# Channel shuffle on one core: five SBUF buffers of 40 KB a partition in place of 38 KB

## The chip, the core and the metric

The kernel runs on one core of one Trainium2 chip. The metric is the device time of one execution in microseconds (us); less is better. Three timed runs of the kernel before gave 316.11, 316.14 and 316.18 us, a median of 316.14 us.

## What is computed

The input `x` is an fp32 tensor of 16 x 64 x 64 pixels with 256 channels each, 67.11 MB. The 256 channels are 8 groups of 32. The reference swaps the two channel axes of every pixel:

```python
x = x.reshape(batch, h, w, groups, channels_per_group)
x = x.transpose(0, 1, 2, 4, 3)
x = x.reshape(batch, h, w, c)
```

There is no arithmetic. Each pixel is 1 KB in and 1 KB out, and 65,536 pixels make 512 pixels for each of the 128 partitions of SBUF. So "q KB a partition" and "q pixels a partition" are the same number here, and the whole job is 512 KB a partition in and 512 KB a partition out.

## The kernel before

The tensor is flattened and cut into pieces. A piece of q KB takes 128 x q pixels that lie together in HBM; partition p gets q of them, so each partition's part is one run of q KB in HBM, and the runs of neighbouring partitions follow one another.

The list `_SLOTS` (line 12) names the pieces. Each inner list is one slot, that is, one pair of buffers: an `in_tile` and an `out_tile`, both as large as the biggest slot. Slot 1 holds two pieces, 4 and 8 KB; slot 2 holds one of 28 KB; then twelve slots hold one piece of 38 KB each; the last holds 16 KB. That makes 16 pieces. `_IN_BUFS` is 2 and `_OUT_BUFS` is 3, so five buffers of 38 KB a partition are in SBUF.

For every piece there are three steps:

- a load (line 55), a DMA from HBM to `in_tile`, issued by SyncE's queue (SP);
- a copy (line 57) on VectorE (DVE), from `in_tile` to `out_tile`, which reads the channels as (group, channel in the group) and writes them as (channel in the group, group);
- a store (line 61), a DMA from `out_tile` to HBM, issued by ScalarE's queue (ACT).

The order on each engine is the order of the program (`manual_schedule`). Nothing else runs but four small memsets at the start. Three waits tie the steps together. A copy waits for its load and, from the fourth slot on, for the store that last used its `out_tile`, three slots back. A load waits from the third slot on for the copies that last read its `in_tile`, two slots back. A store waits for its copy. Loads and stores lie in two hardware queues, q1 and q10, that are served by the same 16 DMA engines; each DMA of 128 partitions gives every engine 8 rows, one descriptor a row, and one small write that raises the semaphore.

Of the kernel before, what the change touches and what calls it, by code (L numbers as in the profile page):

```python
# [1 line left out]

# [4 lines left out]


F32 = mybir.dt.float32
P = 128  # L10

_SLOTS = [[4, 8], [28]] + [[38]] * 12 + [[16]]
_IN_BUFS = 2
_OUT_BUFS = 3


@with_exitstack
def kernel(
    ctx: ExitStack,
    tc: tile.TileContext,  # L20
    x: bass.AP,
    groups: bass.AP,
    out: bass.AP,
):
    nc = tc.nc
    b, h, w, c = x.shape
    G = int(groups)
    CPG = c // G
    assert G * CPG == c
    assert sum(map(sum, _SLOTS)) * P == b * h * w  # L30
    biggest = max(map(sum, _SLOTS))

    x_flat = x.rearrange("b h w c -> (b h w c)")
    out_flat = out.rearrange("b h w c -> (b h w c)")

    in_pool = ctx.enter_context(tc.tile_pool(name="in_pool", bufs=_IN_BUFS))
    out_pool = ctx.enter_context(tc.tile_pool(name="out_pool", bufs=_OUT_BUFS))

    def rows(flat, first, q):

        return flat[first * c : (first + P * q) * c].rearrange("(p f) -> p f", p=P)

    ctx.enter_context(tc.manual_schedule(engines=None))
    first = 0
    for parts in _SLOTS:
        in_tile = in_pool.tile([P, biggest * c], F32, name="in_tile")
        out_tile = out_pool.tile([P, biggest * c], F32, name="out_tile")
        at = 0
        pieces = []
        for q in parts:  # L50
            pieces.append((q, first, slice(at * c, (at + q) * c)))
            first += P * q
            at += q
        for q, start, cols in pieces:
            nc.sync.dma_start(out=in_tile[:, cols], in_=rows(x_flat, start, q))  # L55
        for q, start, cols in pieces:
            nc.vector.tensor_copy(  # L57
                out=out_tile[:, cols].rearrange("p (i j g) -> p i j g", j=CPG, g=G),
                in_=in_tile[:, cols].rearrange("p (i g j) -> p i j g", g=G, j=CPG),
            )  # L60
            nc.scalar.dma_start(
                out=rows(out_flat, start, q), in_=out_tile[:, cols]
            )


# [1 line left out]
_INS = ['x', 'groups']  # L67
_OUTS = [((16, 64, 64, 256), 'float32')]

_NUMBERS = {'groups': 8}  # L70


# [26 lines left out]
```

## Time and profile before

| | |
|---|---|
| timed runs, median | 316.14 us (316.11 to 316.18) |
| profiled execution, first to last instruction (span) | 314.4 us |
| lying around the span, median less span | 1.7 us |
| VectorE busy | 119.0 us, 16 copies |
| one 38 KB copy | 8791 ns |
| bytes moved | 134.22 MB, 427 GB/s over the span |
| DMA queues' share of the 16 engines | q1 49.8%, q10 49.4% |
| 38 KB load, issue to landing | 37.0 us |
| 38 KB store, issue to landing | 42.6 us |

The profile is of one execution of its own, and its page gives the span but no device time beside it; the median of the timed runs is what a new time is held against. A busy share of VectorE is time in which a copy ran. The DMA's busy share is the mean over the core's 16 DMA engines. The trace also holds one record for each DMA packet (here one row of one partition, or one semaphore write) with its start, size and duration; 4608 of them belong to the two queues.

### The profile page before, as it was taken

The page shows a single profiled execution, that of the slowest core. Times are in us where ns is not written, and L with a number is a line of the kernel's source. Part 1 is how long each engine was busy: PE and PEld are TensorE (multiplying, and loading weights), DVE is VectorE, ACT ScalarE, POOL GpSimd, SP SyncE. Part 2 cuts the span into 40 slices and gives each one's busy share as a digit, 9 for nine tenths or more (in the row PEclk, how much of TensorE's full clock was granted, in tenths as well). Part 3 has the DMA queues.
Part 4 walks back from the last instruction along what each step waited for, and adds up shares of the span by engine and source line. Part 5 has one row for each costly group of instructions (what it writes and reads, how often), then busy time and mean ns, then how long its engine had stood idle before and what let it go on. Part 6 is the DMA issues. An engine that isn't in the chain of part 4 may idle for free.

```text
span 314.4 us, 132 instructions
## 1 busy us (share of the span) xinstructions
DVE 119.0 (38%) x16; POOL 0.2 (0%) x4
## 2 busy tenths in 40 slices
DVE  2081907309109109019028028037046055065400
POOL 0000000000000000000000000000000000000000
DMA  7999999999999999999999999999999999999997
GB/s 317 405 441 416 435 416 483 401 465 406 450 421 446 426 436 436 401 470 396 475 396 475 396 470 401 470 401 470 401 450 421 446 426 436 436 417 450 429 421 321
DMA packets 4608, 134.22 MB, mean 427 GB/s; under 512 B 512, under 2 KB 512, under 8 KB 768
## 3 DMA queue, kind: packets, MB, share of 16 engines
q1 hardware_dynamic: 2304, 67.11, 49.8%
q10 hardware_dynamic: 2304, 67.11, 49.4%
HBM read 67.11 MB, written 67.11 MB: 427 GB/s over the span
## 4 chain that ended last, share of the span: by engine, by line
DMA 76%; DVE 19%; issue 0%; SPq 0%; DVEq 0%
DMA in_tile<-in_x_dram 76%; DVE out_tile L57 19%; SPq L55 0%; DVEq L57 0%
## 5 line engine op out<-in xcount | busy, mean ns | idle before, releaser
L57 DVE COPY out_tile<-in_tile 128x9728 f32<-128x9728 f32 (+4 forms) x16 | 119.0, 7440 | 179.4 <-DMA in_tile<-in_x_dram 179.4
L80 POOL MEMSET const-uint8-127<- 128x1 uint8 x1 | 0.1, 103 | 0.0
L80 POOL MEMSET const-bfloat16-1.0<- 128x1 bf16 x1 | 0.1, 102 | 0.0
L80 POOL MEMSET const-float32-1.0<- 128x1 f32 x1 | 0.1, 100 | 0.0
L80 POOL MEMSET const-float32-0.0<- 128x1 f32 x1 | 0.1, 99 | 0.2 <-issue 0.2
## 6 DMA issues: line engine op xcount, KB each, us to landing
in_tile<-in_x_dram SPq DMA_DIRECT2D x12, 4864.0 KB, 37.0
out_dram<-out_tile ACTq DMA_DIRECT2D x12, 4864.0 KB, 42.6
in_tile<-in_x_dram SPq DMA_DIRECT2D x1, 3584.0 KB, 14.7
out_dram<-out_tile ACTq DMA_DIRECT2D x1, 3584.0 KB, 30.9
in_tile<-in_x_dram SPq DMA_DIRECT2D x1, 2048.0 KB, 30.4
out_dram<-out_tile ACTq DMA_DIRECT2D x1, 2048.0 KB, 15.2
in_tile<-in_x_dram SPq DMA_DIRECT2D x1, 1024.0 KB, 5.4
out_dram<-out_tile ACTq DMA_DIRECT2D x1, 1024.0 KB, 25.0
```

Of the source, the lines that this page charges most:

```text
L57: nc.vector.tensor_copy(out=out_tile[:, cols].rearrange("p (i j g) -> p i j g", j=CPG, g=G), in_=in_tile[:, cols].rearrange("p (i g j) -> ...
L80: nc = _bacc.Bacc("TRN2", target_bir_lowering=False, num_devices=1)
```

## The change

One line differs: the twelve slots of 38 KB and the last of 16 KB become eleven slots of 40 KB and a last one of 32 KB. The first three pieces stay.

```diff
-_SLOTS = [[4, 8], [28]] + [[38]] * 12 + [[16]]
+_SLOTS = [[4, 8], [28]] + [[40]] * 11 + [[32]]
 _IN_BUFS = 2
 _OUT_BUFS = 3
```

The five buffers grow from 38 to 40 KB a partition, 200 KB in all. The 16 pieces become 15. The order of the steps, the queues and the waits are the same.

## The prediction

> **What bounds the kernel now.** I read the page's first three parts first. The line of the DMA's busy share is the main one: nine tenths or more (9) in every slice but the first and the last.
>
> ```profile
> span 314.4 us, 132 instructions
> DVE 119.0 (38%) x16; POOL 0.2 (0%) x4
> DMA  7999999999999999999999999999999999999997
> q1 hardware_dynamic: 2304, 67.11, 49.8%
> q10 hardware_dynamic: 2304, 67.11, 49.4%
> ```
>
> The queues' shares add to 99.2% of 314.4 us, or 311.9 us. Only 2.5 us of an engine's span are not transfer. VectorE has 38%. The view of windows (length, VectorE busy, POOL, clock, DMA share, GB/s) shows where the rest lies.
>
> ```profile
> 0.00:1.00 1.00, 0.00 (x0) 0.20 (x4) 1.00 0.00 0
> 1.00:2.00 1.00, 0.00 (x0) 0.00 (x0) 1.00 0.37 45
> 2.00:49.10 47.10, 18.50 (x4) 0.00 (x0) 1.00 1.00 423
> 71.30:278.20 206.90, 79.14 (x10) 0.00 (x0) 1.00 1.00 433
> 278.20:294.50 16.30, 8.72 (x1) 0.00 (x0) 1.00 1.01 434
> 294.50:312.00 17.50, 3.87 (x1) 0.00 (x0) 1.00 0.98 424
> 313.00:314.40 1.40, 0.00 (x0) 0.00 (x0) 1.00 0.00 0
> ```
>
> The DMA stands idle for 1.7 us at the start (first packet at 1.75 us) and 1.2 us at the end (last packet ends at 313.28 us). In between it is full, also in the writes-only stretch after the last load has landed (294.5 on). The timeline says the same from VectorE's side: each 38 KB copy starts 22.99 us after the one before ((278.19 - 71.31) / 9), and VectorE idles about 14.2 us before each, for its load.
>
> ```profile
> 71.31 8.75 DVE L57 COPY out_tile<-in_tile 128x9728 f32<-128x9728 f32 x1 [13.40 <-DMA in_tile<-in_x_dram]
> 278.19 8.73 DVE L57 COPY out_tile<-in_tile 128x9728 f32<-128x9728 f32 x1 [14.21 <-DMA in_tile<-in_x_dram]
> 294.54 3.87 DVE L57 COPY out_tile<-in_tile 128x4096 f32<-128x4096 f32 x1 [7.62 <-DMA in_tile<-in_x_dram]
> ```
>
> The chain that ended last gives VectorE 19%. That is no cost that a faster copy would return: while those copies run, the engines move other rows at full rate. Three things set the time: bytes over the engines' rate, overhead per packet, and idle DMA at the ends.
>
> **The change, term by term.** Bytes: unchanged, 512 KB a partition each way. Head: the pieces of 4, 8 and 28 KB, their addresses, copies and issues are the same, so the 1.7 us before the first packet stay.
>
> Packets: the packet records give 611 ns for a 16 KB row and 1439 ns for a 38 KB row (medians). Neighbouring packets of one engine overlap by some 4 ns in these records: in the steady part a 38 KB row follows the last after 1435 ns and a 16 KB row after 607 ns. The difference, 828 ns for 22,528 bytes, is 0.03675 ns a byte; 16,384 bytes are then 602.2 ns, which leaves 4.8 ns a row that do not grow with its size. A semaphore write takes 6 ns of the engine. One DMA pair less (16 pieces to 15) takes from each engine 8 read rows, 8 write rows and two semaphore writes: 16 x 4.8 + 2 x 6 = 89 ns. By these numbers a steady 38 KB tile is 16 x 1435 + 12 = 22.97 us, against 22.99 measured, and a 40 KB tile will be 16 x 1510 + 12 = 24.18 us. Gain: 0.09 us. A 40 KB row is 5% beyond the largest one in the trace; I take the straight line, since it holds from 4 KB (159 ns) to 38 KB.
>
> Read stalls: write rows show none (38 KB: 1439 median, 1460 longest). Read rows do, early only. The 38 KB reads lose 0.54 us per engine over their median, nearly all of it before 36 us; 0.36 us of that is one event at 33 us, when all 16 engines' reads took 1.7 to 1.85 us. From 36 to 313 us there is next to nothing. These are reads that the change resizes, so this term can go to zero (-0.54) or grow. I take it as unchanged, because the order of rows there (short writes of 4, 8 and 28 KB between long reads) stays, and keep -0.54 and +0.54 as ends.
>
> Row pitch: 40 KB and 32 KB are rounder distances between the rows that the engines read side by side. The nearest row is the last load of before, whose rows are 16 KB apart, a power of two: all its 128 reads took 611 ns, none more. I take 0.
>
> The Trainium skill, "DMA: Bandwidth & Descriptors", section "Latency and other measured facts", speaks against round pitches: it reports 207 GB/s at 512 KiB between rows, 164 at 2 MiB, and 214 with padding. If its mildest loss, 3%, held for the eight 32 KB read rows of 1.21 us, an estimate from that page is +0.3 us and a total of 316.4 us; the 16 KB reads above speak for 0.
>
> Copies, on VectorE: (8791 - 3873) / (9728 - 4096) = 0.873 ns an element, so a 40 KB copy takes 8791 + 512 x 0.873 = 9.24 us and the 32 KB one 3873 + 4096 x 0.873 = 7.45 us. Counted as nothing: 24.18 - 9.24 leaves 14.9 us idle for each tile, and the loads and stores in flight keep the DMA engines full beside it.
>
> Tail: this cover must be checked, since the last copy grows from 3.87 to 7.45 us and nothing loads beside it. A steady tile moves 76 KB a partition in 22.99 us, 0.3025 us a KB. When the last load landed (294.5), writing went on until 313.28: 18.8 us, or 62 KB, of which 16 were the last piece's own and 46 were older stores. These last 13.9 us; the copy and about 1 us from issue to first byte take 4.9; so 9 us of cover were left over (in the packet records the last store's first row starts at 307.99, 8.6 us after it could). Loads and stores alternate row by row, as the packet records show, so the last load's stretch of before loaded 16 and stored 38, and the lead of loads over stores fell from 84 to 62 KB. After, it loads 32 and stores 40: a lead of at least 84 falls to 76, and without the last piece's own 32 leaves 44 KB of older stores, 13.3 us. Less 7.45 + 1, that is a margin of 4.8 us. No gap opens, and the end of the last store with its 1.2 us behind it is as before. If the cover were gone entirely, the cost would be up to 8.5 us.
>
> Waits: an `out_tile` is asked for again three tiles later, 3 x 24.18 = 72.5 us after the copy into it began; its store is issued 9.2 us into that time and lands about 42.6 x 40/38 = 45 us after issue, so some 18 us are left over. A load is issued when the copy two slots back ends; its predecessor then still has some 14 us to go, so SP's queue of loads never runs dry.
>
> Sum: 314.4 - 0.09 = 314.3 us of span; with the same 1.7 us around it, 316.14 - 0.09 = 316.05 us.
>
> **Rivals.** A measurement of this kernel can tell about 0.2%, 0.63 us, from no change.
>
> *Slower: the long reads stay slow.* The first two 38 KB tiles' 256 reads lost 8.6 us together, 33.5 ns each. If 40 KB and 32 KB rows kept meeting this through the run, 96 reads per engine would lose 3.2 us in place of 0.54: +2.7 - 0.09, or 318.7 us. It is visible beyond a mean of 13 ns a read (96 x 13 = 1.26 = 0.63 + 0.54 + 0.09). For it: the stalls of the start are not explained by the trace, and the pitch is rounder. Against it: 38 KB reads lose nothing from 36 us on, 16 KB reads nothing at all. Chance 0.18, nearer to the threshold as likely as at the full price.
>
> *Slower: the tail opens.* The margin goes from about 9 to 4.8 us. If the last load lands over 4.8 us later against the stores than reckoned, every further microsecond is idle DMA: at 6 us, 1.2 us, or 317.3 us. Against it: the same reckoning gives the last stretch of before as 22.97 x 54/76 = 16.3 us, as measured. Chance 0.07.
>
> *Faster: the read stalls go.* Without them, -0.54 - 0.09 gives 315.5 us, just at the threshold; to pass it, the stalls of the first 28 KB reads (0.26 us per engine) would have to shrink too. Chance 0.10.
>
> That the change doesn't do what it says can be left aside: the order of instructions per engine shows eleven copies, loads and stores of 10240 elements and one of 8192, with the rest the same.
>
> **How the numbers follow.** No visible change, 0.65, at 316.05 us; faster 0.10; slower 0.18 + 0.07 = 0.25. The range for 8 in 10: down to 315.4 (stalls gone, and a little more), up to 317.4 (half of the slow reads' price, or the tail open by 1.2 us). Outside lie about 0.05 below and 0.12 above.
>
> **What would show it.** Right: copies of 40 KB that start 24.18 us apart, VectorE idle 14.9 us before each; 433 GB/s in the middle; the last load lands near 290 us (76 KB at 0.3025, 23.0 us, before the last packet's end at 313.2), the last copy takes 7.45 us and the DMA share stays at 1.00 behind it; queue packets 2160 in place of 2304. Wrong: steady tiles over 24.3 us apart (slow reads), a hole in the DMA share between the last copy's start and the last store (tail), or 40 KB rows that take more than 1514 ns each.

## The result and the profile after

The changed kernel's median is 317.85 us (nine runs, 316.32 to 319.23), against 316.17 us for the kernel before (nine runs, 316.02 to 317.47). The ratio is 1.0046, 95% interval 1.0024 to 1.0068. Slower by about half a percent, and with a spread of 2.9 us: the shortest run of the change is near the kernel before, the others trail upward.

The page of the profiled execution after (its device time was 317.25 us), parts 1 to 3:

```profile
span 315.5 us, 126 instructions
DVE 118.9 (38%) x15; POOL 0.2 (0%) x4
DMA  8999999999999999999999999999999999999996
q1 hardware_dynamic: 2160, 67.11, 49.7%
q10 hardware_dynamic: 2160, 67.11, 49.2%
```

The shares of the two queues add to 98.9% of 315.5 us, 312.0 us. It was 311.9 before: the engines have no more to do, on average. The view of windows (columns as before) shows the place:

```profile
73.00:267.00 194.00, 74.04 (x8) 0.00 (x0) 1.00 1.00 433
290.00:312.00 22.00, 7.32 (x1) 0.00 (x0) 1.00 0.99 429
312.00:313.00 1.00, 0.00 (x0) 0.00 (x0) 1.00 0.08 33
313.00:314.00 1.00, 0.00 (x0) 0.00 (x0) 1.00 0.00 0
314.00:315.50 1.50, 0.00 (x0) 0.00 (x0) 1.00 0.00 0
```

The middle runs at 433 GB/s as it did. In the window from 312 to 313 us only 33 KB start (packets are counted where they start). That is one row of 32 KB, on one engine; it ends at 314.19 us. Before, 17 rows of 16 KB start in the same window:

```profile
312.00:313.00 1.00, 0.00 (x0) 0.00 (x0) 1.00 0.65 279
```

The packet records do not name their engine, but each engine's packets follow one another without a gap, so they can be chained. The chains end at these times:

| profile | median of the 16 engines | last but one | last |
|---|---|---|---|
| before | 312.92 | 313.12 | 313.28 |
| after | 312.84 | 313.08 | 314.19 |

The median engine is done 0.08 us sooner than before. The last one lost 1.1 us in six 40 KB reads, at 127, 147, 196, 200, 234 and 249 us, of which the two longest took 353 and 392 ns over the usual 1514 ns. All its 32 KB rows behind them took 1213 ns, so nothing is caught up, and the kernel ends with it.

The timeline after, the copies:

```profile
97.89 9.26 DVE L57 COPY out_tile<-in_tile 128x10240 f32<-128x10240 f32 x1 [14.93 <-DMA in_tile<-in_x_dram]
268.06 9.18 DVE L57 COPY out_tile<-in_tile 128x10240 f32<-128x10240 f32 x1 [15.35 <-DMA in_tile<-in_x_dram]
289.87 7.46 DVE L57 COPY out_tile<-in_tile 128x8192 f32<-128x8192 f32 x1 [12.63 <-DMA in_tile<-in_x_dram]
```

The copies' times are as forecast, and the idle times nearly so. From 97.89 to 268.06 there are seven tiles, 24.31 us each in place of 24.18, just past the 24.3 us that the prediction named as a sign of slow reads: a load is complete when its slowest engine is.

### The profile page after: what moved, and what is told of

It reads as the page before. It is cut to its first block, busy times and chain, and to the rows that moved or that the text cites. A ratio compares the mean times of both kernels' runs of the same rounds, so it can differ in the third digit from the quotient of the medians.

```text
span 315.5 us, 126 instructions
## 1 busy us (share of the span) xinstructions
DVE 118.9 (38%) x15; POOL 0.2 (0%) x4
## 3 DMA queue, kind: packets, MB, share of 16 engines
q1 hardware_dynamic: 2160, 67.11, 49.7%
q10 hardware_dynamic: 2160, 67.11, 49.2%
## 4 chain that ended last, share of the span: by engine, by line
DMA 74%; DVE 19%; SPq 0%; issue 0%; DVEq 0%
DMA in_tile<-in_x_dram 74%; DVE out_tile L57 19%; SPq L55 0%; DVEq L57 0%
## 5 line engine op out<-in xcount | busy, mean ns | idle before, releaser
L57 DVE COPY out_tile<-in_tile 128x10240 f32<-128x10240 f32 (+4 forms) x15 | 118.9, 7926 | 178.4 <-DMA in_tile<-in_x_dram 178.4
```

Source lines behind the costliest of these rows:

```text
L57: nc.vector.tensor_copy(out=out_tile[:, cols].rearrange("p (i j g) -> p i j g", j=CPG, g=G), in_=in_tile[:, cols].rearrange("p (i g j) -> ...
```

## The experiments

The spread is what has to be explained, so the number of runs above 316.6 us stands beside each median (the kernel before has 3 of 108, counting the first result and the chips below on which the change ran too).

**The change again, and three single edits.** The kernel `again` is the change as it is, and so are `again2` to `again4` below, each on another chip.

> The changed kernel once more, beside the kernel before. In the profile after, 15 engines were done by 313.1 us and one at 314.19; that one lost 1.12 us in six 40 KB reads behind 40 us. Theory A (single stalls of one engine's reads, more of them with 40 KB rows): again slower than before, median 316.8 to 318.5 us, with a wide spread, and in the profile one engine ends 0.5 us or more after the mean of the others. Theory B (chance: the nine runs of after met more of a disturbance that has nothing to do with the change): within 0.2% of before, both with the same spread.

`t38_in40` is the kernel before with `biggest = 40`, so that its buffers lie 40 KB apart.

> Tiles of 38 KB in buffers that are spaced 40 KB apart, so only the places in SBUF move to those of the change. If the place in SBUF (200 KB in all) brings the stalls: like the changed kernel, 317 us or more. If the size and pitch of the rows bring them: 316.2 us, like before.

`t40_tail16`:

```diff
-_SLOTS = [[4, 8], [28]] + [[40]] * 11 + [[32]]
+_SLOTS = [[4, 8], [28]] + [[40]] * 11 + [[16]] + [[16]]
```

> Eleven tiles of 40 KB as in the change, but the last 32 KB as two slots of 16 KB. If the large last piece costs (its copy or its store ends late): back to 316.2 us. If the 40 KB rows cost: like the changed kernel, 316.8 to 318.5 us. By the packets alone one DMA pair more than the change is +0.09 us.

`t39` has `[[39]] * 12 + [[4]]` behind the same head.

> Twelve tiles of 39 KB and a last one of 4 KB. If a round row pitch (40 KB, a multiple of 8 KB) brings the stalls: 316.2 us, like before, as 39 KB is an odd number of KB. If longer rows or buffers bring them, whatever their pitch: half of the changed kernel's loss or more, about 317 us.

| kernel | median, range (us) | above 316.6 | ratio (95%) |
|---|---|---|---|
| before, same chip | 316.13, 316.03 to 316.58 | 0 of 29 | |
| again | 316.28, 316.09 to 316.96 | 2 of 11 | 1.0006 (0.9998 to 1.0015) |
| t38_in40 | 316.10, 316.02 to 316.92 | 1 of 11 | 1.0001 (0.9993 to 1.0010) |
| t40_tail16 | 316.21, 316.06 to 317.67 | 4 of 11 | 1.0008 (0.9999 to 1.0017) |
| t39 | 347.89, 344.82 to 349.61 | 6 of 6 | 1.0995 (1.0953 to 1.1036) |

Here the change lost far less than in the first runs: its interval holds 1, and its median lies below the 316.8 us that theory A named. So t38_in40, which is like the kernel before, speaks against the places in SBUF only weakly. The last piece of 32 KB is not needed: with 16 KB pieces last, the runs spread at least as wide. In the profile of t40_tail16 again one engine ends alone, at 314.74 us with the next at 313.21. But 1.1 us of its delay come from three write rows between 280 and 287 us, 77, 464 and 562 ns over the usual; its late reads behind 40 us add 0.19 us.

Neither theory had t39's time; its size brings a loss of its own, and it says nothing on row distance. Its timeline:

```profile
206.59 17.09 DVE L57 COPY out_tile<-in_tile 128x9984 f32<-128x9984 f32 x1 [8.69 <-DMA in_tile<-in_x_dram]
232.41 17.11 DVE L57 COPY out_tile<-in_tile 128x9984 f32<-128x9984 f32 x1 [8.73 <-DMA in_tile<-in_x_dram]
```

A copy of 39 pixels takes 17.1 us; 38 take 8.8 and 40 take 9.2. The Trainium skill, "VectorE: DVE Perf Modes", section "What auto-detection actually checks", names a condition for the double rate of a one-source copy: the outermost dimensions of source and destination must both be even, or equal. In the trace the source of this copy is 8 x 32 x 39 elements, outermost last, and the destination is one run of 9984; the time of one element, 1.71 ns in place of 0.90, agrees with a loss of the double rate. With the last copies that long, the tail that the prediction feared does open (windows of t39):

```profile
171.00:310.00 139.00, 86.71 (x6) 0.00 (x0) 1.00 1.00 399
317.00:330.00 13.00, 12.95 (x2) 0.00 (x0) 1.00 0.19 79
```

**Other sizes.** All sizes are even from here on: `[[32]] * 14 + [[24]]`, `[[36]] * 13 + [[4]]`, `[[34]] * 13 + [[30]]` behind the same head.

> The changed kernel a third time. So far its runs lie between 316.09 and 319.23 us, with a shortest time like that of before and a long upper side: single packets of one engine stall, and that engine ends last. Theory A (40 KB rows meet such stalls more often than 38 KB rows): median 0.1 to 1.7 us above before, most of the spread above 316.4 us. Theory B (chance): the same spread as before.

> Fourteen tiles of 32 KB and one of 24 KB: rows lie 32 KB apart, a power of two, and are shorter. If a round row pitch brings the stalls: slower than the changed kernel, 317 us or more, wide spread. If long rows bring them: no stalls, a narrow spread, and only the packets' price, three DMA pairs more than the change: 3 x 0.09 = 0.27 us, about 316.3 us.

> Thirteen tiles of 36 KB and one of 4 KB. Row pitch 36 KB is a multiple of 4 KB, between 38 (of 2 KB) and 40 (of 8 KB). If pitch brings the stalls: between before and the changed kernel. If long rows bring them: like before or better, 316.2 us, by the packets +0.09 us on before.

> Thirteen tiles of 34 KB and one of 30 KB. Row pitch 34 KB is a multiple of 2 KB only, like 38 KB. Both theories: narrow spread, 316.1 to 316.3 us (one DMA pair more than... the count is 17 pieces, so +0.09 us on before). If its last piece of 30 KB matters, the end of the profile shows a hole in the DMA share.

| kernel | median, range (us) | above 316.6 | ratio (95%) |
|---|---|---|---|
| before, same chip | 316.12, 316.02 to 316.36 | 0 of 35 | |
| again2 | 316.80, 316.15 to 318.73 | 7 of 11 | 1.0028 (1.0014 to 1.0042) |
| t32 | 316.47, 316.39 to 318.28 | 1 of 12 | 1.0015 (1.0006 to 1.0024) |
| t36 | 316.22, 316.16 to 318.83 | 2 of 12 | 1.0010 (0.9997 to 1.0024) |
| t34 | 316.22, 316.17 to 316.37 | 0 of 11 | 1.0003 (0.9994 to 1.0011) |

The theory of chance falls: the change is slower than before here too, with the kernel before entirely below 316.4 us. The shortest runs of t34 and t36 lie 0.15 us above before's, in the direction of the packets' price, and t32's 0.37. The order 34, 38 (narrow) and 36, 40 (wide) made the distance between rows a suspect: 34 and 38 KB are multiples of 2 KB only. But 32 KB, the roundest, is narrow but for one run.

**Row length against row distance.** Behind the head, each partition now owns one long run in HBM, and a piece takes the next part of each run. The length of a row and the distance between the rows come apart:

```diff
+        whole = flat[begin_px * c : (begin_px + P * _MAIN[2]) * c].rearrange("(p f) -> p f", p=P)
+        return whole[:, o * c : (o + q) * c]
```

> The changed kernel's pieces, with another layout in HBM: behind the first 40 KB each partition owns one run of 472 KB, and a 40 KB piece takes the next 40 KB of each run. The rows stay 40 KB long but lie 472 KB apart (a multiple of 8 KB, as 40 is). If the long rows bring the stalls (row theory): median 316.3 to 317.5 us, wide. If the distance between rows brings them by its power of two (pitch theory): the same. Says nothing alone, it is the partner of the next.

> Rows of 40 KB as in the change, 470 KB apart (a multiple of 2 KB only, as 38 and 34 are); the last piece is 30 KB, with 2 KB more behind it. Pitch theory: narrow, 316.1 to 316.3 us, no run above 316.6. Row theory: wide, median 316.3 to 317.5 us, a third or more of the runs above 316.6.

> Rows of 38 KB as before, 472 KB apart (a multiple of 8 KB). Pitch theory: wide, median 316.3 us or more, a third of the runs above 316.6. Row theory: narrow, 316.1 us.

> Rows of 38 KB, 470 KB apart (a multiple of 2 KB only); the last piece 14 KB, with 2 KB more behind it. Both theories: narrow, 316.1 to 316.3 us. If it is wide, the large distance itself matters and neither theory holds as it stands.

| kernel | median, range (us) | above 316.6 | ratio (95%) |
|---|---|---|---|
| before, same chip | 316.12, 316.02 to 319.13 | 1 of 35 | |
| p40m472 | 316.23, 316.16 to 317.07 | 2 of 12 | 1.0002 (0.9986 to 1.0018) |
| p40m470 | 316.07, 316.03 to 318.81 | 1 of 12 | 1.0000 (0.9979 to 1.0020) |
| p38m472 | 316.27, 316.01 to 317.06 | 5 of 12 | 1.0005 (0.9988 to 1.0021) |
| p38m470 | 316.29, 316.13 to 319.12 | 1 of 13 | 0.9998 (0.9982 to 1.0014) |

This looked a little like the distance (7 of 24 runs above 316.6 us at 472 KB, 2 of 25 at 470 KB), but every interval holds 1, and the change itself did not run on this chip. The profile of p38m470 fell on its longest run, 319.12 us, and its windows show the same end as the change, drawn out:

```profile
312.00:313.00 1.00, 0.00 (x0) 0.00 (x0) 1.00 0.72 279
313.00:314.00 1.00, 0.00 (x0) 0.00 (x0) 1.00 0.10 39
314.00:315.00 1.00, 0.00 (x0) 0.00 (x0) 1.00 0.07 29
315.00:316.00 1.00, 0.00 (x0) 0.00 (x0) 1.00 0.04 14
```

Fifteen engines are done by 313.26 us, one at 316.16. So rows of 38 KB can meet the same fate; p38m472, also with 38 KB rows, has 5 of its 12 runs above 316.6 us.

**VectorE's share.** 35 of the 37 late reads behind 40 us that are counted below lay inside a copy, so the copy was moved to ScalarE, or made twice.

```diff
-            nc.vector.tensor_copy(
+            nc.scalar.copy(
```

```diff
+            for _ in range(2 if q >= 38 else 1):
```

> The changed kernel once more, as the partner of the other kernels on this chip. Median 0.05 to 0.7 us above before, and a fifth or more of the runs above 316.6 us.

> The change, with ScalarE making the copies in place of VectorE. In the profiles so far, behind 40 us and before the last copy ends, 28 of the 30 stalled reads (over 30 ns above the usual) lay wholly inside a VectorE copy, which covers 46% of the reads' time. If VectorE's work in SBUF is one half of the cause: no such stalls, all runs within 0.3 us of the shortest (a copy of ScalarE that takes up to 14 us for 40 KB stays hidden; above that the end opens). If the reads' own place in the load is the cause (the first three rows): the same wide spread as the changed kernel.

> The change, with every 40 KB copy made twice on VectorE (18.5 us of a 24.2 us tile). If VectorE's work in SBUF is one half of the cause: stalls over rows 0 to 5 of a load in place of 0 to 2, about twice as many, median 0.3 to 2 us above the changed kernel on this chip. If the place in the load is the cause: the same as the changed kernel; the last copy is not doubled, so the end does not open.

> The kernel before, with every 38 KB copy made twice on VectorE (17.6 us of a 23.0 us tile). If stalls need both the rounder row distance and VectorE's work: like before, 316.1 to 316.3 us, narrow. If VectorE's work alone brings them: wide, 316.5 us or more.

| kernel | median, range (us) | above 316.6 | ratio (95%) |
|---|---|---|---|
| before, same chip | 316.14, 316.03 to 317.44 | 1 of 14 | |
| again3 | 317.32, 316.28 to 319.36 | 8 of 9 | 1.0051 (1.0032 to 1.0070) |
| act40 | 356.84, 355.97 to 357.61 | 4 of 4 | 1.1281 (1.1259 to 1.1302) |
| twice40 | 353.83, 351.09 to 354.60 | 6 of 6 | 1.1177 (1.1147 to 1.1207) |
| twice38 | 330.64, 330.55 to 330.94 | 4 of 4 | 1.0455 (1.0439 to 1.0470) |

The question stays unanswered, because a copy of 17.5 to 18.6 us costs far more than any stall. Neither theory had this. (again3 was also slower than forecast: 1.18 us above before, for 0.05 to 0.7.) The windows of before in the steady part; then those of twice38, in the steady part and near the end, where the DMA share falls:

```profile
94.30:278.20 183.90, 70.39 (x9) 0.00 (x0) 1.00 1.00 433
```

```profile
123.40:268.40 145.00, 105.77 (x12) 0.00 (x0) 1.00 1.00 412
303.00:310.00 7.00, 7.00 (x1) 0.00 (x0) 1.00 0.59 253
```

In the steady part of twice38 the DMA engines are full and yet slower: the read rows take 1439 ns as ever, the write rows 1574 (median). In twice40 and act40 the write rows take 1738 and 1749 ns for the usual 1514, and t39, with its 17 us copies, has 1654 for 1476; in these three some reads are slow too. The writes are slow outside the copies too: in the six steady tiles of twice38 those between the copies average 1602 to 1619 ns and those inside one 1578 to 1591. So there it is not the copy's traffic in SBUF. In twice40 and act40 the writes inside a copy are the slower ones (averages of 1731 to 1810 ns a tile, against 1573 to 1776 between the copies), so a part of that traffic is not excluded. What a longer copy does change is when a store is issued, and with it the order of rows on each engine. Before, every tile has one place with two reads in a row and one with two writes; in twice38's steady part reads and writes alternate without either. That this order is the cause is a reading of the records that no run tested.

**The last pair.** `p40m474` has the head 4, 8, 26, rows of 40 KB, 474 KB apart, and 34 KB last.

> The change's 15 pieces with eleven of 40 KB, but the head 4, 8 and 26 KB and the last piece 34 KB, and behind the first 38 KB each partition owns one run of 474 KB: rows of 40 KB, 474 KB apart (a multiple of 2 KB only). If the distance between rows decides: narrow, median 316.0 to 316.2 us, no more than one run in ten above 316.6, and one DMA pair less than before is worth 0.09 us, so it may come out at 316.03 us, the best of all. If the 40 KB rows decide: like the changed kernel.

> The changed kernel, the partner on this chip: rows of 40 KB, 40 KB apart. Median 0.1 to 1.5 us above before, a fifth or more of the runs above 316.6 us.

Before on this chip: 316.25 us (316.02 to 316.95, 1 of 21 above 316.6). p40m474: 316.74 us (316.36 to 317.07, 8 of 11), ratio 1.0017 (1.0008 to 1.0026). again4: 316.52 us (316.14 to 317.24, 5 of 11), ratio 1.0010 (1.0001 to 1.0018). The distance theory in its simple form falls: 474 KB is a multiple of 2 KB only, and 8 of 11 runs are above 316.6 us, against 5 of 11 for the change. Its profile (316.94 us) again has one late engine, 313.89 us against 313.08 for the next; this one was held by a single 40 KB read of 2.8 us at 33 us, among the first. As the first pieces of p40m474 differ from the change's, the pair is not as clean as its expectation took it to be.

**What the records say over all of them.** Two readings come from the profiles of all kernels with copies of the usual length. First, for the 15 profiled executions whose own device time is known, that time is the end of the last engine's last packet plus 2.93 to 3.10 us, whatever the kernel:

```
kernel       median engine   last engine   device time
p40m470          312.87         313.11        316.04
t34              313.11         313.29        316.27
again            312.86         313.26        316.32
again2           312.77         313.74        316.80
after            312.84         314.19        317.25
t40_tail16       313.08         314.74        317.67
t36              313.05         315.79        318.75
p38m470          312.99         316.16        319.12
```

The median engine stays within 0.5 us (312.71 to 313.19 us); the last one spreads over 3 us and carries the time with it. Second, where rows stall. Each engine serves loads and stores in turn, row by row. Once a tile the store queue's turn is only the 9 ns semaphore write that ends a store, and two reads follow each other. Behind 40 us, in these profiles and that of before, 30 of the 37 reads that took over 30 ns more than usual were the second of such a pair:

```
read row comes after                      over 30 ns late   all
a write row, not wholly inside a copy            2         14,007
a write row, inside a VectorE copy               5          6,198
a read row, inside a VectorE copy               30          2,749
a read row, not wholly inside a copy             0             41
```

(A semaphore write between the two rows is not counted as a row.) That is 1.1% after a read against 0.03% after a write. In the steady tiles the second read starts 3 to 6 us after a copy begins, so it runs within the copy; that is why VectorE looked guilty. A copy alone explains few of them: inside a copy, reads that follow a write were late in 0.08% of cases. In twice38, from 75 us on, no read follows a read, and all its 1,136 reads of 38 KB took 1439 ns, though 576 of them ran inside a copy. (Three of its reads near 50 us were late, behind two write rows and a semaphore write.) Whether a pair stalls without a copy stays open, since only 41 pairs lay outside one. The one stall of all sixteen engines near 33 us, in the profile before, is the second of two reads too.

Write rows stall too, though the prediction found none in the profile before: five of 27,776 behind 40 us were over 30 ns late, in t36 and t40_tail16. They are long ones, 77 to 710 ns, and three of the five, among them the longest two, were the second of two writes.

## Why the prediction was wrong

The forecast was no visible change, 316.05 us, range 315.4 to 317.4; the first measurement was 317.85. Over the five comparisons the change cost 0.06, 0.10, 0.28, 0.46 and 0.51%, with 28 of its 51 runs above 316.6 us. The four later medians, 316.28 to 317.32 us, lie inside the range, so that the first lay outside was in part the draw; that the change costs time is not.

- *Packets*: right. A 40 KB row took 1514 ns as on the straight line, the queues moved 2160 packets each, and the median engine ended 0.08 us sooner, where 0.09 was reckoned. (16 x 1510 + 12 makes a tile 24.17 us, not 24.18; nothing hangs on it.)
- *Copies*: right, 9245 and 7455 ns.
- *Tail*: right. The last load's copy started at 289.87 us, for 290 forecast, and no hole followed it. Its rival did not happen in the change; t39 and twice38 show what it looks like.
- *Row pitch at 0*: the 32 KB reads took 1213 ns to the last one, so the 0.3 us that the prediction estimated for them from "DMA: Bandwidth & Descriptors" did not show. For the 40 KB rows, the runs with other distances neither clear nor convict the distance.
- *Read stalls*: the step that failed, "I take it as unchanged". The prediction priced this term as a mean over the engines, 0.54 us. After, that mean is 0.64 us, so the term grew by only 0.10. But the end is set by the slowest of the 16, and of the 1.6 us that all 16 together lost more than before, about 1.0 sat on one. Before, the last engine's lag behind the median was 0.36 us; after, 1.35. "Next to nothing" behind 36 us was true for the mean, while the engine that ended last before had a single 67 ns stall at 168 us, a first sign of what came.
- *The slower rival*, reads that stay slow, had the right rows but the wrong form. It priced 33.5 ns on every read of all engines; what came in the profile after were six single stalls of 33 to 392 ns on one engine. The faster rival's price, all stalls gone, rests on the same mean.

What stays open is why rows of 40 KB draw more of these stalls than rows of 38. The last piece of 32 KB is not needed for the long runs (t40_tail16); the places in SBUF are made unlikely by t38_in40 but not excluded. Row distance alone is contradicted by p40m474, row length alone is doubtful after p40m470. No version beat the kernel before: p40m470 has a median 0.05 us lower, well inside its interval.

## What to carry to other kernels

When the DMA engines are full throughout, their mean says what the work costs, but the kernel ends with the slowest of the 16: look at the last microsecond of the windows for a single row, chain the packets by engine, reads and writes alike, and price stalls on one engine, not on the mean. Such stalls differ from execution to execution, and the change's cost went from 0.06 to 0.51% between the five sets of runs, so a change in tile size needs several runs of both kernels, and the share of long runs belongs beside the median. Where a copy like this one may handle an even or an odd number of pixels, take the even one, and do not count a copy as free merely because VectorE has idle time.

## What was not expected of the hardware

- One engine of 16 collects stalls: up to 3.2 us behind the median engine (p38m470), with the other fifteen within 0.3 us of it. They struck a read that follows a read 1.1% of the time, other reads 0.03%, and five writes.
- Copying an odd number of pixels took 17.1 us for 39, against 9.2 us for 40.
- With copies of 17 to 19 us where a tile took 23 to 24 us before, write rows became 9 to 16% slower, inside the copies and between them (1574 for 1439 ns, 1749 for 1514), and the kernel 4.6 to 12.8% slower, though the engine that copies still waited for its loads.
